# Group 2's mixer projection in feature pairs with the block operands beside it, group 0's final norm inside one projection, and the mixer constants at another address

## The chip, the cores and the metric

The kernel runs on one core of a Trainium2 chip. The metric is device time in microseconds from the start of one launch to its end. The kernel before was timed in three runs; a further execution was recorded by the hardware profiler, and it is that execution whose rows are shown here. Engines carry the profile's names: PE is TensorE (matmuls) and PEld its weight loads, DVE is VectorE, ACT is ScalarE, POOL is GpSimd, SPq is the queue in which SyncE issues DMAs.

## What is computed

The reference is one inference step of a two-layer decoder on 1040 prompt positions (16 learned meta tokens and 1024 own ones) and 8 decode tokens, with 1024 features. Layer 0 mixes tokens by a causal convolution, layer 1 by an RWKV-7 recurrence; each is followed by a squared-ReLU MLP with 4096 hidden features. Cut to what matters:

```python
def _trunk(h, ...):
    for i in range(DEPTH):                       # DEPTH = 2
        hn = _rmsnorm(h, norm_mix[i])
        if i % N_MIXERS == 0:
            out, buf = _conformer_conv(hn, ...)
        else:
            out, sh, S = _rwkv7(hn, ...)         # ends with ((yn + bonus) * g) @ w_o
        h = h + out
        h = h + _sqrelu_mlp(_rmsnorm(h, norm_mlp[i]), w_mlp_in[i], w_mlp_out[i])
    return _rmsnorm(h, norm_final), ...

def _sqrelu_mlp(h, w_in, w_out):
    return jnp.square(jax.nn.relu(h @ w_in)) @ w_out
```

The change touches what stands behind the recurrence: the projection by `w_o` with its residual add, the preparation of layer 1's MLP, the final norm of the first third of the positions, and the place in memory of some constants of layer 1's mixer.

## The kernel before

**Layout.** Features lie on the 128 partitions, in `KT` = 8 blocks, and tokens along the free axis. A product in full precision is three matmuls (`mm3`, lines 209 to 213): every operand is split into a high part (a cast on ACT, lines 159 and 177) and a low part (a subtraction, line 160 on DVE for activations, line 182 on POOL for weights in four pieces of 256). A dense product of one 128-feature column is 8 blocks times three, 24 matmuls.

**Stages.** Layer 0's convolution and MLP come first, then layer 1's mixer in four groups with its inputs (`mixer_in`), beside which a serial recurrence over 17 chunks runs. The rest works on three groups of positions, `G2` = 328, 352 and 352 wide, called 0, 1 and 2:

- `mixer_out(g)` (lines 1614 to 1627) loads the residual `h1` and the mixer's output `z` (eight `zr` loads, each split), takes eight weight columns of `w_o` one after the other, multiplies each with `z` into a bank `ps_oo`, adds the bank to the residual (line 1625), squares the sum for the norm (line 276), and calls `fill` in the middle of each column and after it, so that other work is woven in.
- Group 0 goes through `mixer_out(0)` and its own MLP (`mlp`), with the end of the recurrence woven in.
- Groups 1 and 2 go through `mixer_out(1)` and `mixer_out(2)` and then share one MLP, `strassen_mlp`, which computes a block of two hidden columns for two groups with seven half products in place of eight. Their operands are `b11` and `b21` (group 1's own activations) and `b22`, `n1`, `t2`, `t3`, `m4`, which `strassen_acts` forms from both groups' residuals (lines 1695 to 1721). The order of the products on PE is `a11` by `b11`, `a12` by `b21`, `s2` by `t2`, `n1` by `n1`, `s3` by `t3`, `s4` by `b22`, `a22` by `m4`. Each half product is 12 matmuls. The weight operands of a block come from `strassen_weights`, four DVE operations (lines 1730 to 1733).
- `strassen_acts` runs in program order after all of `mixer_out(2)`. For each of the four feature pairs (i, i + 4) it forms the four differences on DVE (lines 1711 to 1714), `b22` (1715 and 1716), and splits the four.
- `final(g)` is the final norm of a group: squares, a scaling by the norm's weights, row sums, and for every 128 positions eight transposes into two banks `pf` (line 1662), two evictions into an output tile `ot` (DVE line 1667, ACT line 1665) and one DMA. `final(0)` is woven into `mixer_out(1)` and `mixer_out(2)` by `filler(4 * KT, ..., FB)`, 32 points for a weight of `FB` = 40 units of which the generator has 22; its rest is drained after `mixer_out(2)`.

**What sets the order.** The program is traced in the order of the text and then placed by a planner that simulates the engines: each instruction has a priority by its place in the text, and the planner gives an engine the first one in priority that is ready in its simulated time. On the chip every engine and every DMA queue then works strictly in the planned order. So an instruction can be planned ahead of others that stand before it in the text; the operands of `strassen_acts` and the loads for `mixer_out` are such cases.

**Buffers.** Weight tiles as they come from memory (`raw`) rotate through a `Ring` of `raw_a` (2 buffers) and `raw_f` (3), and `ot` takes its tile from the same ring. PSUM banks at that point are six `mm`, one `w` (`psw2`) and one `x`; `final` uses `w` for both halves of a tile if the group is 0 or 1. Temporaries `t1` and `t2` have three buffers each. `residp` holds group 0's residual and is reused by `t3`; `actp2` holds group 2's `z` and is reused by `m4` and `b22`; `actp3` holds `n1` and `t2`. A pool that reuses an address waits for the last reader of what lay there.

**The mixer's constants.** The pool `mixc` (from line 787) holds `hsum`, `hsel`, `hspread`, `half`, `negs` and `omka`, 5.3 KB for a partition. It is opened first in the stack `ld`, ahead of `hnp` (`hx`, `xx`), `lorap`, `pr` and `mixp` (lines 819 to 822). When the mixer ends, `ld` is closed and the pools of the last stage are laid over it from the same lowest address, `raw_f` first.

Of the kernel before, what the change touches and what calls it, by code (L numbers as in the profile page):

```python
# [48 lines left out]
def hybrid_step(tc, x_prompt, x_sample, state_conv, state_shift, state_wkv, meta_tokens,  # L49
# [10 lines left out]
    with ctx:  # L60
# [724 lines left out]
        ld = ctx.enter_context(ExitStack())  # L785
        mixc = pool(ld, "mixc", 1)
# [32 lines left out]
        hnp = pool(ld, "hnp", 1)  # L819
        lorap = pool(ld, "lorap", 1)  # L820
        pr = pool(ld, "pr", 1)
        mixp = pool(ld, "mixp", 1)
# [777 lines left out]
        with ExitStack() as l1:  # L1600
# [13 lines left out]
            def mixer_out(g, residp, actp, fill, add):  # L1614
                lo, n = G2[g]
                h1 = hl[g] = residp.tile([P, KT, cur["wide"]], F32, name=f"h1_{g}", tag="h")
                nc.sync.dma_start(h1[:, :, :n], d_h[:, :, lo:lo + n])
                z = new_act(actp, f"z{g}", cur["wide"])
# [4 lines left out]
                for m in range(KT):  # L1623
                    ps = dense(load_col(rwkv_w_o[0], m, f"wo{g}_{m}", nc.gpsimd), z, n, f"oo{g}_{m}", fill)
                    nc.vector.tensor_add(h1[:, m, :n], h1[:, m, :n], ps[:, :n])
                    add(m, h1[:, m, :n])
                    fill()

            def final(g):
# [24 lines left out]
                for j, i in enumerate(starts):  # L1654
# [3 lines left out]
                    ot = cur["raw"].tile([P, D], F32, name=f"ot{g}_{i}", tag="raw")  # L1658
                    for hf in range(2):
                        pt = bank(f"pf{g}{i}{hf}", "w" if g < 2 or hf else "mm")  # L1660
# [34 lines left out]
            def strassen_acts(first, h2, n, own, shared, last):  # L1695

                ah, al, h1 = first[3], first[4], first[1]
                parts = {}
                for q, (pl, tag) in enumerate(((own, "t1"), (own, "t2"), (shared, "h"))):
                    t = pl.tile([P, KT, cur["wide"]], F32R, name=f"sa{q}", tag=tag)  # L1700
                    parts[q] = t[:, :HT, :n], t[:, HT:, :n]
                zh, zl = new_act(last, "sa3", cur["wide"])
                parts[3] = zh[:, :HT, :n], zl[:, :HT, :n]
                b22 = zh[:, HT:, :n], zl[:, HT:, :n]
                for i in range(HT):
                    lo, hi = h2[:, i, :], h2[:, HT + i, :]
                    x = tt(f"sx{i}", "t2")[:, :n]
                    nc.scalar.activation(x, lo, AF.Copy, scale=gam(i))
                    t = [tt(f"st{q}{i}", "t1")[:, :n] for q in range(3)] + [tt(f"st3{i}", "t2")[:, :n]]
                    stt = nc.vector.scalar_tensor_tensor  # L1710
                    stt(t[0], h1[:, i, :], gam(i), x, op0=ALU.mult, op1=ALU.subtract)
                    stt(t[2], hi, gam(HT + i), x, op0=ALU.mult, op1=ALU.subtract)
                    stt(t[1], hi, gam(HT + i), t[0], op0=ALU.mult, op1=ALU.add)
                    stt(t[3], h1[:, HT + i, :], gam(HT + i), t[1], op0=ALU.mult, op1=ALU.subtract)
                    nc.scalar.activation(b22[0][:, i], hi, AF.Copy, scale=gam(HT + i))
                    stt(b22[1][:, i], hi, gam(HT + i), b22[0][:, i].bitcast(F32), op0=ALU.mult, op1=ALU.subtract)
                    for q in range(4):
                        split(parts[q][0][:, i], parts[q][1][:, i], t[q], nc.vector)
                low = lambda k: [t[:, k:k + HT, :n] for t in (ah, al)]
                return dict(b11=low(0), b21=low(HT), b22=b22, n1=parts[0], t2=parts[1], t3=parts[2], m4=parts[3])  # L1720
# [112 lines left out]
            cur.update(rings((raw_a, raw_f), (wsp_a, wsp_f)))  # L1833
            cur["mm"] = Ring((cur["mm"], 4), (pool(lp, "psum2", 2, space=PSUM), 2))
# [6 lines left out]
            fill, rest = filler(4 * KT, ([ranked(FN, final(0))], FB))  # L1841
# [54 lines left out]
```

## Time and profile before

| what | value |
|---|---|
| three runs, median (lowest to highest) | 2796.94 us (2789.36 to 2797.69) |
| the profiled execution's own time | 2799.78 us |
| its span, on which all rows are placed | 2797.9 us |
| mean granted TensorE clock | 0.966 |
| busy POOL, share of the span | 1731.6 us, 62% |
| busy ACT, share of the span | 1405.6 us, 50% |
| DMA moved | 428.31 MB, mean 153 GB/s |

The times of rows are microseconds from the start of the span. A timeline row reads: start, length, engine, line, operation, output from inputs, shapes, count, and in brackets how long the engine had been idle and what released it. A row of consecutive instructions is merged, so a DMA issue of 24 us in the queue SPq is the time in which a run of issues held the queue, with their waits. A row of the groups reads: line, engine, operation, names, shapes, count, busy us, mean ns, and idle time before. Lines are those of helpers where a helper records the operation: 159 and 160 are `split`, 165 `load_raw`, 177 and 182 `load_w`, 211 to 213 `mm3`, 266 the sums of `mean_bcast`, 288 the accumulation of squares, 295 the reciprocal of `rstd_of`.

### The profile page before, as it was taken

Reading aid. Unit: us, or ns where it says so; the run is one execution under the profiler, and the core shown is the slowest. Engines: PE = TensorE matmul, PEld = TensorE weight load, DVE = VectorE, ACT = ScalarE, POOL = GpSimd, SP = SyncE. Lnnn points to the kernel's source line nnn. Section 1 sums busy time; section 2 is a strip of 40 time slices with the busy share of each in tenths; the row PEclk is TensorE's granted clock in tenths of the full one; section 3 lists DMA queues with packets and bytes.
Section 4 is the critical chain, followed back from the end, with each engine's and each line's share of the span. In section 5 each row is a group of like instructions: output and inputs, shape, how many; then the busy total and the mean of one; then the engine's idle time right before and its main releaser. Section 6 shows DMA issues by size and latency. Waiting matters only on the chain.

```text
span 2797.9 us, 54227 instructions
## 1 busy us (share of the span) xinstructions
PE 2603.5 (93%) x20362; PEld 2508.0 (90%) x20362; DVE 2050.5 (73%) x3860; ACT 1405.6 (50%) x2616; POOL 1731.6 (62%) x2287
## 2 busy tenths in 40 slices
PE   8998999999998999988898899878899989999998
PEld 7998999999998999978787788768889989999998
DVE  5999999996457464786888786777797667555565
ACT  5545444544355444565657666754444544333333
POOL 6686877887786354645434344647558775666563
PEclk9999999999999999999999899989999999999999
DMA  6573544454444556678878787796557452222221
GB/s 186 160 194 91 160 136 136 131 181 136 138 132 143 154 155 177 191 199 197 225 201 203 201 215 183 190 234 179 142 136 230 139 153 68 76 68 79 73 69 64
DMA packets 659284, 428.31 MB, mean 153 GB/s; under 512 B 126840, under 2 KB 609208, under 8 KB 659022
## 3 DMA queue, kind: packets, MB, share of 16 engines
q1 hardware_dynamic: 652780, 421.93, 54.2%
q10 hardware_dynamic: 6018, 2.89, 0.4%
q8 instruction: 160, 2.62, 0.4%
q14 instruction: 102, 0.84, 0.1%
q0 software_dynamic: 224, 0.03, 0.0%
HBM read 353.03 MB, written 72.66 MB: 152 GB/s over the span
## 4 chain that ended last, share of the span: by engine, by line
PE 61%; DVE 16%; DMA 8%; POOL 6%; ACT 5%; issue 4%; SPq 1%; ACTq 0%; POOLq 0%; DVEq 0%
PE out L212 4%; PE out L213 4%; PE out L211 4%; PE ps_in L212 4%; PE ps_in L213 4%; PE ps_in L211 4%; PE os L212 3%; PE os L213 3%; PE os L211 3%; POOL wo_lo L182 2%; POOL wi_lo L182 2%; PE su L211 1%; PE su L213 1%; PE su L212 1%; DVE cv L552 1%
## 5 line engine op out<-in xcount | busy, mean ns | idle before, releaser
L182 POOL TENSOR_TENSOR wo_lo<-wo_raw,wo_hi 128x256 fp32r<-128x256 f32 x544 | 427.9, 820 | 190.0 <-ACT wo_hi L177 176.9
L182 POOL TENSOR_TENSOR wi_lo<-wi_raw,wi_hi 128x256 fp32r<-128x256 f32 x472 | 366.1, 809 | 163.0 <-ACT wi_hi L177 160.5
L552 DVE SCALAR_TENSOR_TENSOR cv<-u,wdw,cv 128x352 f32<-128x352 f32 (+2 forms) x720 | 376.6, 572 | 0.7
L211 PE MATMUL out<-hh,wo_hi 128*128 128x348 f32 (+2 forms) x1024 | 335.1, 331 | 21.7 <-DVE h L382 9.1
L211 PE MATMUL ps_in<-m_h,wi_hi 128*128 128x348 f32 (+2 forms) x1024 | 330.4, 323 | 5.2 <-DVE h L382 3.1
L212 PE MATMUL out<-hh,wo_lo 128*128 128x348 f32 (+2 forms) x1024 | 332.5, 325 | 2.2 <-DVE wo_lo L182 2.2
L213 PE MATMUL out<-hl,wo_hi 128*128 128x348 f32 (+2 forms) x1024 | 328.7, 324 | 2.0 <-DVE hl L160 2.0
L212 PE MATMUL ps_in<-m_h,wi_lo 128*128 128x348 f32 (+2 forms) x1024 | 328.6, 322 | 0.9 <-POOL wi_lo L182 0.8
L213 PE MATMUL ps_in<-m_l,wi_hi 128*128 128x348 f32 (+2 forms) x1024 | 328.1, 321 | 0.2
L382 DVE TENSOR_TENSOR h<-h,out 128x348 f32<-128x348 f32 (+2 forms) x512 | 249.9, 503 | 66.5 <-PE out L213 66.4
L177 ACT CAST wo_hi<-wo_raw 128x1024 fp32r<-128x1024 f32 x152 | 159.2, 1049 | 207.3 <-PE ps_in L213 115.8
L177 ACT CAST wi_hi<-wi_raw 128x1024 fp32r<-128x1024 f32 x128 | 134.2, 1048 | 236.7 <-PE out L213 113.4
L211 PEld LDWEIGHTS out<-hh,wo_hi 128*128 128x128 f32 x1024 | 195.9, 192 | 30.1 <-DVE h L382 11.4
L211 PEld LDWEIGHTS ps_in<-m_h,wi_hi 128*128 128x128 f32 x1024 | 193.3, 189 | 8.4 <-issue 3.3
L212 PEld LDWEIGHTS out<-hh,wo_lo 128*128 128x128 f32 x1024 | 196.7, 192 | 4.2 <-DVE wo_lo L182 2.9
L213 PEld LDWEIGHTS out<-hl,wo_hi 128*128 128x128 f32 x1024 | 195.3, 192 | 3.2 <-DVE hl L160 2.7
L212 PEld LDWEIGHTS ps_in<-m_h,wi_lo 128*128 128x128 f32 x1024 | 193.0, 189 | 2.8 <-POOL wi_lo L182 1.7
L213 PEld LDWEIGHTS ps_in<-m_l,wi_hi 128*128 128x128 f32 x1024 | 192.3, 188 | 1.4 <-DVE m_l L305 0.7
L1803 DVE TENSOR_TENSOR h<-h,os 128x352 f32<-128x352 f32 x256 | 127.4, 515 | 57.9 <-PE os L213 57.2
L212 PE MATMUL os<-hhs,wos_lo 128*128 128x352 f32 x512 | 165.2, 323 | 0.0
L213 PE MATMUL os<-hls,wos_hi 128*128 128x352 f32 x512 | 164.2, 323 | 0.0
L211 PE MATMUL os<-hhs,wos_hi 128*128 128x352 f32 x512 | 156.1, 323 | 0.0
(498 smaller groups left out, 8036.1 us busy)
## 6 DMA issues: line engine op xcount, KB each, us to landing
wi_raw<-in_w_mlp_in_dram SPq DMA_DIRECT2D x128, 512.0 KB
wo_raw<-in_w_mlp_out_dram SPq DMA_DIRECT2D x128, 512.0 KB
wk_raw<-in_rwkv_w_k_dram SPq DMA_DIRECT2D x32, 512.0 KB
wr_raw<-in_rwkv_w_r_dram SPq DMA_DIRECT2D x32, 512.0 KB
wv_raw<-in_rwkv_w_v_dram SPq DMA_DIRECT2D x32, 512.0 KB
d_ab<-ab SPq DMA_DIRECT2D x32, 512.0 KB
ws_raw<-in_w_mlp_in_dram SPq DMA_DIRECT2D x32, 512.0 KB
wos_raw<-in_w_mlp_out_dram SPq DMA_DIRECT2D x32, 512.0 KB
```

The lines of the kernel that those rows point to most:

```text
L177: nc.scalar.copy(hi[:, :a * b], raw[:, :a * b])
L182: eng_lo.tensor_sub(lo[:, cs], raw[:, cs], hi[:, cs].bitcast(F32))
L211: nc.tensor.matmul(ps, w[0], act[0], start=first, stop=False, **kw)
L212: nc.tensor.matmul(ps, w[1], act[0], start=False, stop=False, **kw)
L213: nc.tensor.matmul(ps, w[0], act[1], start=False, stop=last, **kw)
L382: nc.vector.tensor_add(hv[:, 4 * i + m, :], hv[:, 4 * i + m, :], ps[:, :n])
L552: nc.vector.scalar_tensor_tensor(acc[m][:, :n], ug[:, m, j:j + n], wdw[:, m, j:j + 1], acc[m][:, :n], op0=ALU.mult, op1=ALU.add)
L1803: nc.vector.tensor_add(hv[:, 4 * i + m, :], hv[:, 4 * i + m, :], ps[:, :n])
```

## The change

It has three parts.

1. **Group 2's projection in pairs.** `mixer_out` takes an order of columns and a hook. For group 2 the order is 0, 4, 1, 5, 2, 6, 3, 7, nothing is woven in, and after the second column of each pair the hook forms `n1`, `t2`, `t3` for that pair. `strassen_acts` becomes two functions: `early`, the hook, and `late`, which after the norm's statistics forms `b22` and then `m4`. As the difference behind `t2` is no longer kept, `m4` starts from its two split parts, added on POOL.
2. **Group 0's final norm within `mixer_out(1)`.** The weaving has 16 points and a weight of 25, and the rest is drained right behind `mixer_out(1)`. Its output tiles come from a new pool `outp` with one buffer, and the first half of each tile's transposes uses the `mm` banks.
3. **Constants.** `hnp`, `lorap`, `pr` and `mixp` are opened ahead of `mixc`.

```diff
@@ the pools of the mixer
         ld = ctx.enter_context(ExitStack())
+        hnp = pool(ld, "hnp", 1)
+        lorap = pool(ld, "lorap", 1)
+        pr = pool(ld, "pr", 1)
+        mixp = pool(ld, "mixp", 1)
         mixc = pool(ld, "mixc", 1)
...
-        hnp = pool(ld, "hnp", 1)
-        lorap = pool(ld, "lorap", 1)
-        pr = pool(ld, "pr", 1)
-        mixp = pool(ld, "mixp", 1)
@@ mixer_out
-            def mixer_out(g, residp, actp, fill, add):
+            def mixer_out(g, residp, actp, fill, add, order=range(KT), early=None):
+                ready = None
...
+                if early:
+                    ready = early(h1)
...
-                for m in range(KT):
+                for i, m in enumerate(order):
                     ps = dense(load_col(rwkv_w_o[0], m, f"wo{g}_{m}", nc.gpsimd), z, n, f"oo{g}_{m}", fill)
                     nc.vector.tensor_add(h1[:, m, :n], h1[:, m, :n], ps[:, :n])
-                    add(m, h1[:, m, :n])
+                    add(i, h1[:, m, :n])
+                    if ready:
+                        ready(m)
                     fill()
@@ final
-                    ot = cur["raw"].tile([P, D], F32, name=f"ot{g}_{i}", tag="raw")
+                    ot = (cur["raw"] if g else outp).tile([P, D], F32, name=f"ot{g}_{i}", tag="raw")
                     for hf in range(2):
-                        pt = bank(f"pf{g}{i}{hf}", "w" if g < 2 or hf else "mm")
+                        pt = bank(f"pf{g}{i}{hf}", "w" if hf or g == 1 else "mm")
@@ strassen_acts, new
+                def early(h2):
+                    for q, pl, tag in (("n1", own, "t1"), ("t2", own, "t2"), ("t3", shared, "h")):
+                        room(q, pl, tag)
+
+                    def ready(m):
+                        if m < HT:
+                            return
+                        i = m - HT
+                        lo, hi = h2[:, i, :n], h2[:, m, :n]
+                        x = tt(f"sx{i}", "t2")[:, :n]
+                        nc.scalar.activation(x, lo, AF.Copy, scale=gam(i))
+                        t = {q: tt(f"st{q}{i}", "t1")[:, :n] for q in ("n1", "t2", "t3")}
+                        stt(t["n1"], h1[:, i, :], gam(i), x, op0=ALU.mult, op1=ALU.subtract)
+                        stt(t["t2"], hi, gam(m), t["n1"], op0=ALU.mult, op1=ALU.add)
+                        stt(t["t3"], hi, gam(m), x, op0=ALU.mult, op1=ALU.subtract)
+                        for q in t:
+                            split(ops[q][0][:, i], ops[q][1][:, i], t[q], nc.vector)
+                    return ready
+
+                def late(h2, pl):
+                    zh, zl = new_act(pl, "sa3", cur["wide"])
+                    ops["m4"] = zh[:, :HT, :n], zl[:, :HT, :n]
+                    b22 = ops["b22"] = zh[:, HT:, :n], zl[:, HT:, :n]
+                    for i in range(HT):
+                        hi = h2[:, HT + i, :n]
+                        nc.scalar.activation(b22[0][:, i], hi, AF.Copy, scale=gam(HT + i))
+                        stt(b22[1][:, i], hi, gam(HT + i), b22[0][:, i].bitcast(F32), op0=ALU.mult, op1=ALU.subtract)
+                    for i in range(HT):
+                        t4 = tt(f"st4{i}", "t2")[:, :n]
+                        nc.gpsimd.tensor_add(t4, ops["t2"][0][:, i].bitcast(F32), ops["t2"][1][:, i].bitcast(F32))
+                        stt(t4, h1[:, HT + i, :], gam(HT + i), t4, op0=ALU.mult, op1=ALU.subtract)
+                        split(ops["m4"][0][:, i], ops["m4"][1][:, i], t4, nc.vector)
+                return ops, early, late
@@ the last stage
+            outp = pool(l1, "outp", 1)
...
-            fill, rest = filler(4 * KT, ([ranked(FN, final(0))], FB))
+            fill, rest = filler(2 * KT, ([ranked(FN, final(0))], 25))
             add, sums = sums_of(1)
             mixer_out(1, residp2, actp, fill, add)
-            g1 = group(1, actp, hidp, sums)
-            add, sums = sums_of(2)
-            mixer_out(2, residp2, actp2, fill, add)
             for _ in rest:
                 pass
+            g1 = group(1, actp, hidp, sums)
             n = G2[2][1]
+            ops, early, late = strassen_acts(g1, n, actp3, residp)
+            add, sums = sums_of(2)
+            mixer_out(2, residp2, actp2, lambda: None, add, [m for i in range(HT) for m in (i, i + HT)], early)
             rs = rstd_of(mean_bcast(sums, n, "m12"), n, 0, "m12", "rsm", 2)
-            ops = strassen_acts(g1, hl[2][:, :, :n], n, actp3, residp, actp2)
+            late(hl[2], actp2)
```

More of the change, by code (lines that the diff above doesn't have):

```diff
@@ L1693, in hybrid_step, with strassen_acts, room @@
             gam = lambda k: vec("norm_mlp", KT + k)
-            def strassen_acts(first, h2, n, own, shared, last):
+            def strassen_acts(first, n, own, shared):
                 ah, al, h1 = first[3], first[4], first[1]
-                parts = {}
-                for q, (pl, tag) in enumerate(((own, "t1"), (own, "t2"), (shared, "h"))):
+                low = lambda k: [t[:, k:k + HT, :n] for t in (ah, al)]
+                ops = dict(b11=low(0), b21=low(HT))
+                stt = nc.vector.scalar_tensor_tensor
+                def room(q, pl, tag):
@@ L1700, in strassen_acts @@
                     t = pl.tile([P, KT, cur["wide"]], F32R, name=f"sa{q}", tag=tag)
[L1701 to L1718, printed above, removed]
@@ L1719, in strassen_acts @@
-                low = lambda k: [t[:, k:k + HT, :n] for t in (ah, al)]
-                return dict(b11=low(0), b21=low(HT), b22=b22, n1=parts[0], t2=parts[1], t3=parts[2], m4=parts[3])
+                    ops[q] = t[:, :HT, :n], t[:, HT:, :n]
+                def early(h2):
[15 more added lines that the diff above has]
+                    return ready
```

## The prediction

> **What bounds the kernel now.** The first view is the page: the head, the busy shares, the slices.
>
> ```profile
> span 2797.9 us, 54227 instructions
> ...
> PE 2603.5 (93%) x20362; PEld 2508.0 (90%) x20362; DVE 2050.5 (73%) x3860; ACT 1405.6 (50%) x2616; POOL 1731.6 (62%) x2287
> ...
> PE   8998999999998999988898899878899989999998
> ```
>
> TensorE is busy 93% of the span, and the change removes no matmul. So only the holes of TensorE beside the touched code can give time. A busy share hides part of a hole, because ends of matmuls are modelled and a matmul at half clock counts as busy; I therefore count matmuls per stretch. The second view is the table of windows, over the two places that the tail edits touch (columns: length, then busy us and count of PE, PEld, DVE, ACT, POOL, then the granted clock, DMA share, GB/s).
>
> ```profile
> 2244.00:2256.00 12.00, 9.10 (x41) 8.43 (x40) 4.06 (x6) 4.37 (x6) 6.21 (x9) 0.72 0.76 222
> ...
> 2300.00:2336.00 36.00, 27.58 (x129) 24.06 (x128) 30.70 (x44) 18.66 (x36) 20.23 (x23) 0.86 0.19 57
> 2336.00:2372.00 36.00, 36.00 (x227) 36.00 (x227) 25.08 (x42) 15.64 (x27) 24.97 (x31) 1.00 0.25 74
> ```
>
> The last row is full speed: 227 matmuls in 36 us, 0.159 us each. In 2300 to 2336 there are 129, 98 fewer: 98 x 0.159 = 15.6 us lost. Eight of the 129 are the slower sums of squares (rows under hole B: a pair takes 0.75 to 0.86 us with its end, two others 0.159 + 0.32), four pairs that take about 1 off: **15 us** in round. In 2244 to 2256 there are 41, eight of them transposes (row under hole A: 1.05 us for four): 33 x 0.159 + 2.1 = 7.3 us of work in 12, so **4.7 us** lost. The rest of the span after 2336 is full and is not touched.
>
> **Hole A, 2244 to 2256, and the first group's final norm.** The timelines of SyncE's queue and of TensorE name the cause.
>
> ```profile
> 2207.91 8.73 SPq L165 DMA_DIRECT2D wo_raw<-in_rwkv_w_o_dram  x3
> 2216.74 24.25 SPq L1621 DMA_DIRECT2D zr<-d_z  x14
> 2241.04 1.05 SPq L165 DMA_DIRECT2D wo_raw<-in_rwkv_w_o_dram  x2
> ...
> 2247.53 0.34 SPq L1669 DMA_DIRECT2D out_dram<-ot  x1
> ```
>
> ```profile
> 2246.97 0.66 PE L211 MATMUL ps_oo<-z_h,wo_hi 128*128 128x352 f32 x1 [2.76 <-ACT wo_hi L177]
> 2249.70 1.05 PE L1662 MATMUL pf<-ident,h 128*128 128x128 f32 x4
> ```
>
> The fifth weight column of group 1's projection is issued at 2241.04, behind fourteen `zr` loads that hold the in-order queue for 24.25 us, six of them group 2's. Its buffer comes from a ring of five, which in program order reads column 0, 1, 2, `ot`, 3, 4, `ot`, 5: the output tile `ot` takes a slot, so column 4 must wait until column 0's is free. The change gives the first group's `ot` a pool of its own (`outp`, one buffer). Column 4 then takes the fifth slot, and one reuse less stands before it; it ranks before group 2's `zr`, so the planner can issue it ahead of them. Moving the final norm's instructions removes and adds none: 24 transposes, six evictions and three output transfers stay; they are spread over 16 fill points at 25/16 instead of 32 at 40/32, so the first `ot` comes at fill point 5 instead of 6. Half of the transposes go to the `mm` banks instead of the single `w` bank.
>
> `outp` adds a wait: the second `ot` can be written only when the first transfer has landed. Behind that waiting eviction on VectorE and ScalarE stand the residual adds and weight casts. Tiles lie 5 units apart, at 25/16 per fill point 3.2 points, and a point is 12 matmuls, 1.9 us: 6.1 us apart. The nearest landings of 512 KB are these two in the chain.
>
> ```profile
> 2241.04 4.80 DMA wo_raw<-in_rwkv_w_o_dram
> ```
>
> ```profile
> 1838.15 7.33 DMA wo_raw<-in_rwkv_w_o_dram
> ```
>
> At 4.80 us the wait is nothing, at 7.33 it is 1.2 us twice, covered by free `mm` banks. So hole A is worth 0 (the order stays) to 4.7; I take **-4.5**, since the slot that blocked is the edit's own.
>
> **Hole B, 2300 to 2336, and the feature pairs.** The projection of group 2 ends at T = 2300.7, where the sums start.
>
> ```profile
> 2300.70 0.75 PE L266 MATMUL st_m<-acc_m,ones_d 128*128 128x352 f32 x2
> 2302.78 0.86 PE L266 MATMUL st_m<-acc_m,ones_d 128*128 128x352 f32 x2 [1.33 <-DVE acc_m L288]
> ...
> 2324.90 0.55 PE L211 MATMUL su<-sa,ws_hi 128*128 128x352 f32 x1
> ...
> 2334.91 0.43 PE L211 MATMUL su<-sa_h,wb_hi 128*128 128x352 f32 x1 [0.62 <-DVE u L1779]
> ```
>
> The third product of the block (`s2` by `t2`) starts at T + 24.2. By TensorE alone it could start after eight sums (about 2 us) and 24 matmuls (3.8): T + 5.8. VectorE, which forms the operands, has two holes before T and after them none that counts until 2327:
>
> ```profile
> 2278.26 0.65 DVE L1711 SCALAR_TENSOR_TENSOR st<-h,pvec,sx 128x352 f32<-128x352 f32 x1 [3.52 <-ACT sx L1708]
> ...
> 2286.96 1.08 DVE L1730 SCALAR_TENSOR_TENSOR wsa<-ws_raw 128x512 f32<-128x512 f32 x1 [4.54 <-POOL wo_lo L182]
> ...
> 2327.78 0.58 DVE L160 TENSOR_TENSOR hls<-p,hhs 128x352 fp32r<-128x352 f32 x1 [1.08 <-ACT hhs L159]
> ```
>
> That is 8.06 us free, because with columns in order 0 to 7 the first pair (0, 4) is complete only after five columns of 24 matmuls (3.8 us each). In order 0, 4, 1, 5, ... pairs are complete after 2, 4, 6, 8, so the first three are 11.4, 7.6 and 3.8 us earlier and fall into these gaps. What still ran on VectorE after 2300, from the groups by shape:
>
> ```profile
> L160 DVE TENSOR_TENSOR sa<-st,sa 128x352 fp32r<-128x352 f32 x9 | 6.0, 684 | 0.0
> L1716 DVE SCALAR_TENSOR_TENSOR sa_l<-h,pvec,sa_h 128x352 fp32r<-128x352 f32 x4 | 3.3, 815 | 0.0
> L160 DVE TENSOR_TENSOR sa_l<-st,sa_h 128x352 fp32r<-128x352 f32 x4 | 3.1, 784 | 0.0
> L295 DVE RECIPROCAL rs_m<-sd_m 128x352 f32<-128x352 f32 x1 | 2.3, 2339 | 0.0
> L1713 DVE SCALAR_TENSOR_TENSOR st<-h,pvec,st 128x352 f32<-128x352 f32 x3 | 2.2, 733 | 0.0
> L1714 DVE SCALAR_TENSOR_TENSOR st<-h,pvec,st 128x352 f32<-128x352 f32 x3 | 2.2, 726 | 0.0
> L1711 DVE SCALAR_TENSOR_TENSOR st<-h,pvec,sx 128x352 f32<-128x352 f32 x2 | 1.6, 806 | 0.0
> ...
> L1712 DVE SCALAR_TENSOR_TENSOR st<-h,pvec,sx 128x352 f32<-128x352 f32 x2 | 1.1, 571 | 0.0
> ```
>
> The first, fifth, seventh and eighth rows are `n1`, `t2`, `t3`: 16 instructions, 10.9 us. After the change the last pair alone is left, five instructions (its `n1` needs only column 3): 5 x 0.72 = 3.6 us, so `t2` is ready near T + 5 and the third product loses almost nothing. The late part then holds the end: 3.6, the reciprocal 2.3, `b22` 3.3, `m4` 3.1 + 4 x 0.73 = 6.0, and the first hidden tile's add, scale and split, about 2.2: 17.4 us, so `m4` near T + 18. Its product is due at T + 2 + 72 x 0.159 = T + 13.5. The gap of some 4.5 us can take 24 matmuls of the next block (3.8 us), as the trace does before. I leave 5 us of the 15: **-10**.
>
> ScalarE's count is unchanged. Four additions on GpSimd that rebuild `t2` are new, 1.2 us each by this row:
>
> ```profile
> L288 POOL TENSOR_TENSOR acc_m<-acc_m,sq 128x352 f32<-128x352 f32 x1 | 1.2, 1225 | 0.0
> ```
>
> They stand among the weight splits: 4.9 us, and behind them `wb_lo` and the next block's `wa_lo`. GpSimd's own timeline has a hole there:
>
> ```profile
> 2303.28 3.92 POOL L182 TENSOR_TENSOR wt_lo<-wsb,wt_hi 128x256 fp32r<-128x256 f32 x4
> 2312.06 2.02 POOL L182 TENSOR_TENSOR wb_lo<-ws_raw,wb_hi 128x256 fp32r<-128x256 f32 x2 [4.87 <-ACT wb_hi L177]
> ```
>
> Its 4.87 us are the cover; without it the last product waits up to 4.9 us.
>
> **The price of sharing.** The same operation costs twice as much while GpSimd works:
>
> ```profile
> 2293.64 1.06 DVE L1713 SCALAR_TENSOR_TENSOR st<-h,pvec,st 128x352 f32<-128x352 f32 x1
> ...
> 2308.16 0.57 DVE L1713 SCALAR_TENSOR_TENSOR st<-h,pvec,st 128x352 f32<-128x352 f32 x1
> ```
>
> GpSimd was splitting at 2293 and idle at 2308. Moved before T, all 24 operations can cost about 1 us. Eleven early ones more, at 1.0, are 11 us against 8.06 free; 3 us overflow past T, and up to 5 more where the late ones lose their quiet stretch. So B lies between -3 and -14.
> The Trainium skill says in "SBUF — State Buffer", section "Who interferes with whom", that a VectorE instruction with two SBUF inputs contends with a GpSimd instruction that reads SBUF, and that whichever starts first has the pair until it ends. The two rows above agree (1.06 against 0.57 us); by that rule every moved operation pays the long price, which is the second rival.
>
> **Part C, the mixer's constants.** Only addresses change: `mixc` (5.3 KB by its shapes) goes from below `hnp` to above `mixp`. The tail's first raw weight buffers reuse the lowest addresses. Before, they wait for the constants' last reader, after it for `hx`:
>
> ```profile
> L1135 PEld LDWEIGHTS pk<-rk,hsum x64: 186/189/394, 1162.0 to 1829.1; 128*128 128x128 f32 x64
> ```
>
> ```profile
> L890 DVE SCALAR_TENSOR_TENSOR mx<-xx,pvec,hx x96: 382/484/1282, 886.1 to 1750.4; 128x256 f32<-128x256 f32 x48, 128x272 f32<-128x272 f32 x24, 128x264 f32<-128x264 f32 x24
> ```
>
> So three loads can leave up to 79 us earlier. They now hold SyncE here:
>
> ```profile
> 1837.67 4.21 SPq L165 DMA_DIRECT2D wo_raw<-in_rwkv_w_o_dram  x3
> ```
>
> ```profile
> 1837.55 3.39 PE L1286 MATMUL A<-xa,bk 128*128 128x256 f32 x8 [7.84 <-DMA bk<-d_ab]
> ```
>
> TensorE's 7.84 us wait ends before these loads are issued, so it stays; behind them only SyncE's 4.21 us goes, from the gate operands' loads. I take **-2**, with -8 (wait and queue shortened) and +6 (one load in front of the chain, near the 7.33) as ends.
>
> **The sum.** The profiled execution takes 2799.78 us, its span of 2797.9 and 1.9 around it. 2799.8 - 4.5 - 10 - 2 = 2783.3. Its 2799.78 lies 2.84 above the median of the three runs, 2796.94 (2789.36 to 2797.69), so the median forecast is **2780**.
>
> **Rivals.** (1) *The queue order stays*: fourteen `zr` still hold SyncE, the same wait takes A's place. For it: the planner chose that order once; against: the freed slot. A = 0: 2785. (2) *VectorE remains the bound* through sharing: B = -3, A = -4.5, C = 0: 2789. For it: the doubled durations; against: the quiet 4.87 us. (3) *Both holes close and the mixer's end loosens*: -4.7 - 14 - 6 = -25: 2772. (4) *The change does not do what it says*: the planner had already drawn eleven operand operations before T, and gains nothing more: 2796. (5) *Slower*: the three early `wo_raw` loads are put ahead of the recurrence's loads in 1750 to 1830, in a serial chain. 3 x 7.33 = 22 us, and after each hole a lower clock as in hole A (0.72 over 12 us, at most 3.4 us, 2 taken) makes 28; with A and B, +13: 2810. It decides once more than 14.5 us of that delay reach the chain. For it: the DMA share of 1.00 in 1820 to 1860; against: the low rank of these loads.
>
> ```profile
> 1820.00:1860.00 40.00, 24.69 (x371) 20.09 (x370) 25.66 (x54) 23.05 (x53) 22.48 (x28) 0.83 1.00 273
> ```
>
> **How the numbers follow.** Forecast 0.42, rivals (1) 0.18, (2) 0.20, (3) 0.08, (4) 0.05, (5) 0.07. The bound of 0.3%, about what a measurement can tell from no change, is 8.4 us: faster means below 2788.5. The forecast but 0.02, rival (1) but 0.01, (3) and 0.08 of (2) are faster: 0.73; (5) is slower: 0.07; the rest 0.20. The range 2768 to 2793 leaves out half of (3), (4), (5) and a little of (2): under 0.2.
>
> **What would show it.** A: `wo_raw` for column 4 issued before group 2's `zr`, and some 75 matmuls in the 12 us where there were 41. B: `s2` by `t2` within 8 us of the last projection matmul instead of 24.2, and VectorE's two holes gone. C: `wo_raw` issued between 1750 and 1835. Wrong would be: VectorE without a gap yet ending as late after T; or a new wait of `ot` on its transfer; or group 0's projection starting later than before.

## The result and the profile after

| kernel | median (lowest to highest), runs | profiled execution, span |
|---|---|---|
| before | 2793.81 us (2789.36 to 2797.69), 4 | 2799.78 us, 2797.9 us |
| changed | 2773.59 us (2773.24 to 2776.21), 4 | 2773.24 us, 2771.5 us |

The ratio is 0.993, with a 95% interval of 0.9911 to 0.995: faster, by some 20 us. The execution of before whose rows were shown lies 6 us over its median, so the two traces are 26.5 us apart. The page of the changed kernel, its head, busy shares and TensorE's slices:

```profile
span 2771.5 us, 54241 instructions
...
PE 2596.3 (94%) x20362; PEld 2500.8 (90%) x20362; DVE 2064.6 (74%) x3860; ACT 1405.7 (51%) x2616; POOL 1738.0 (63%) x2291
...
PE   8998999999998999997898889979989999999998
```

TensorE has the same 20362 matmuls. VectorE has the same count too, yet 14.1 us more of busy time: its mean instruction became dearer. Most of that comes with part C: VectorE is busy 2060.9 to 2065.4 us in the traces with C and 2049.9 to 2054.7 in those without. The windows of the changed kernel over the two places (columns as before: length, busy us and count of PE, PEld, DVE, ACT, POOL, clock, DMA share, GB/s):

```profile
2212.00:2224.00 12.00, 12.00 (x84) 11.96 (x83) 8.73 (x14) 9.14 (x20) 9.72 (x12) 1.00 0.56 160
2224.00:2236.00 12.00, 12.00 (x82) 11.72 (x81) 8.51 (x14) 7.74 (x13) 10.73 (x13) 1.00 0.88 270
...
2276.00:2312.00 36.00, 27.27 (x147) 25.02 (x146) 32.18 (x42) 18.80 (x37) 26.78 (x29) 0.95 0.15 44
2312.00:2348.00 36.00, 34.49 (x216) 34.20 (x215) 21.61 (x40) 13.32 (x23) 23.04 (x28) 1.00 0.25 74
```

The first two rows are group 1's projection: where before had 41 matmuls at a clock of 0.72 there are now 84 and 82 at 1.00. Hole A is gone. The last two rows begin with the end of group 2's projection: 147 matmuls where before had 129, then 216 where before had 227. Hole B became shallower and longer. The cause of the first is in SyncE's queue:

```profile
2201.90 8.60 SPq L1624 DMA_DIRECT2D zr<-d_z  x6
2210.55 3.59 SPq L165 DMA_DIRECT2D wo_raw<-in_rwkv_w_o_dram  x2
2216.83 2.36 SPq L1624 DMA_DIRECT2D zr<-d_z  x3
```

The run of fourteen `zr` that held the queue for 24.25 us is broken up; six of group 1's `zr` are followed by two `wo_raw`, and only then come the next `zr`.

**Where the time went.** All fourteen traces of this study were cut at three points that every kernel has: the first matmul of group 0's projection (`ps_oo`), the last output matmul of group 0's MLP, and T, the last matmul of group 2's projection (2300.5 in before). Microseconds, worked out from the first and last starts of these tiles, good to 0.1:

| kernel | parts in it | first `ps_oo` at | to end of group 0's MLP | to T | T to end | `s2` by `t2`, after T |
|---|---|---|---|---|---|---|
| before | none | 1856.4 | 370.0 | 74.1 | 497.4 | 24.4 |
| changed | A B C | 1845.3 | 363.5 | 66.8 | 495.9 | 12.6 |
| `only_a` | A | 1844.7 | 365.0 | 66.8 | 492.8 | 20.6 |
| `only_b` | B | 1852.8 | 367.7 | 73.3 | 495.7 | 15.2 |
| `only_c` | C | 1844.8 | 361.6 | 72.9 | 498.5 | 25.1 |
| `a_and_b` | A B | 1853.0 | 367.5 | 66.8 | 494.7 | 13.5 |
| `a_and_c` | A C | 1849.0 | 364.9 | 66.8 | 492.9 | 20.6 |
| `b_and_c` | B C | 1840.6 | 360.4 | 73.6 | 496.0 | 15.6 |

The 26.4 us are 11.1 ahead of group 0's projection, 6.5 in its MLP, 7.3 on the way to T, and 1.5 behind T. So part C, which was priced at 2 us, and part A carry the result; part B, priced at 10, nearly nothing.

How far one trace can be trusted shows in the last stretch: `before` and `only_c`, the changed kernel and `a_and_b`, `only_b` and `b_and_c`, `only_a` and `a_and_c` each share TensorE's planned order behind T, and the two of a pair lie 1.1, 1.2, 0.3 and 0.1 us apart there. The 1.5 us behind T are hardly more than that.

### The profile page after: what moved, and what is told of

It is laid out like the page before. It is cut to its first block, busy times and chain, and to the rows that moved or that the text cites. A ratio compares the mean times of both kernels' runs of the same rounds, so it can differ in the third digit from the quotient of the medians.

```text
span 2771.5 us, 54241 instructions
## 1 busy us (share of the span) xinstructions
PE 2596.3 (94%) x20362; PEld 2500.8 (90%) x20362; DVE 2064.6 (74%) x3860; ACT 1405.7 (51%) x2616; POOL 1738.0 (63%) x2291
## 4 chain that ended last, share of the span: by engine, by line
PE 62%; DVE 17%; DMA 9%; issue 4%; ACT 4%; POOL 3%; SPq 1%; POOLq 0%; ACTq 0%; DVEq 0%
PE ps_in L212 5%; PE ps_in L213 4%; PE out L212 4%; PE ps_in L211 4%; PE out L213 4%; PE out L211 4%; PE os L211 3%; PE os L213 3%; PE os L212 3%; DVE cv L552 2%; PE su L213 1%; PE su L212 1%; PE su L211 1%; PE A L1286 1%; DMA wr_raw<-in_rwkv_w_r_dram 1%
## 5 line engine op out<-in xcount | busy, mean ns | idle before, releaser
L211 PE MATMUL out<-hh,wo_hi 128*128 128x348 f32 (+2 forms) x1024 | 332.8, 328 | 18.7 <-DVE h L382 7.7
```

The source lines that it names most:

```text
L211: nc.tensor.matmul(ps, w[0], act[0], start=first, stop=False, **kw)
```

## The experiments

### Each part alone, and each left out

`only_c` moves the four pools ahead of `mixc`. All kernels made for this study drain the rest of group 0's final norm right behind `mixer_out(1)`, as the changed kernel does and before doesn't, also those called without A. That alone is small: to T the kernels without a piece of A take 72.9 to 73.6 us, before 74.1. `only_a` is before with the new pool, the banks and the weaving:

```diff
-                    ot = cur["raw"].tile([P, D], F32, name=f"ot{g}_{i}", tag="raw")
+                    ot = (cur["raw"] if g else outp).tile([P, D], F32, name=f"ot{g}_{i}", tag="raw")
...
-                        pt = bank(f"pf{g}{i}{hf}", "w" if g < 2 or hf else "mm")
+                        pt = bank(f"pf{g}{i}{hf}", "w" if hf or g == 1 else "mm")
...
+            outp = pool(l1, "outp", 1)
...
-            fill, rest = filler(4 * KT, ([ranked(FN, final(0))], FB))
+            fill, rest = filler(2 * KT, ([ranked(FN, final(0))], 25))
```

`only_b` has the pair order with `early` and `late` and nothing else. `a_and_b` is the changed kernel with the pools in their old order, `a_and_c` the changed kernel with the old `strassen_acts` and its call, `b_and_c` the changed kernel with `ot` in the ring, the old banks and the old weaving.

> The kernel before with part C alone, the constants above mixp. Theory of the two traces: the address change brings most of the gain, because group 0's projection started 11.1 us earlier and its sums 14.5 us earlier: 2793.8 - 14 = 2780 us, with the first ps_oo near 1845. Rival, the sizes of the prediction: C brings 2 us, 2792, and the early stages owe their shift to chance in one profiled execution. Second rival, the parts do not add: anything between, with holes A and B unlike both kernels.

> The kernel before with part A alone: group 0's final norm with its own output pool, mm banks and 16 weaving points. Theory of the two traces: between the end of group 0's MLP and the end of group 2's projection 7.4 us went, so 2793.8 - 6 = 2788 us, with the load of column 4 ahead of group 2's zr and no wait of PE on a weight cast there. Rival, the queue order stays: 2793 us and the wait of 2.8 us is still there.

> The kernel before with part B alone: feature pairs, early and late operands. Theory of the two traces: from the end of the projection to the first product of s2 by t2 it is still 19 us, VectorE is the bound, and B brings 1 to 2 us: 2792 us. Rival, the size of the prediction: B brings 10 us, 2784 us, and its loss in the changed kernel comes from meeting A or C.

> The changed kernel with the pools of the mixer in the old order, so A and B without C. Theory of the two traces, with parts that add: 2793.8 - 6 - 1.5 = 2786 us. If C brings only 2 us, as the prediction has it: 2776 us. If the parts do not add, it lies apart from the sum of only_a and only_b by more than 4 us.

> The changed kernel with the projection of group 2 and the operands as before, so A and C without B. Theory: only_a and a_and_b say that the feature pairs cost some 3 us once the final norm is out of the way (492.8 us from the last projection matmul to the end without them, 494.7 with them), because VectorE is bound before and after T; then this beats the changed kernel by 2 to 5 us, 2770 us. Rival, B is worth its 1 to 2 us here as well: 2775 us.

> The changed kernel with group 0's final norm as before, so B and C without A. Theory of parts that add: the stretch from the end of group 0's MLP to the last projection matmul is 73 us in the kernels without A and 66.8 in those with it, so this loses 6 to 7 us against the changed kernel: 2780 us. Rival, A owes its gain to chance in the early stages: 2774 us, and the stretch is 67 us here.

Measured, each against runs of before taken beside it:

| kernel | median us, runs | before us | ratio, 95% |
|---|---|---|---|
| `only_c` | 2781.11, 6 | 2791.64 | 0.9955, 0.9937 to 0.9972 |
| `only_a` | 2778.33, 6 | 2791.64 | 0.9948, 0.9933 to 0.9963 |
| `only_b` | 2790.25, 12 | 2791.64 | 0.9993, 0.9982 to 1.0004 |
| `a_and_b` | 2784.59, 12 | 2791.64 | 0.9975, 0.9966 to 0.9984 |
| `a_and_c` | 2771.96, 6 | 2793.29 | 0.9924, 0.9908 to 0.9939 |
| `b_and_c` | 2777.34, 6 | 2793.29 | 0.9948, 0.9928 to 0.9969 |

A alone and C alone are each faster, B alone can't be told from before. `only_c`, `only_b` and `b_and_c` came within 3 us of their first theory; `only_a` came 10 us below its 2788, in part for a reason behind T that is told below. The saving of `a_and_b` is 7.7 us less than the sum of those of `only_a` and `only_b` (7.05 against 13.31 and 1.39), so A and B don't add. The intervals of `a_and_b` and `only_a` don't meet: B put on top of A alone made the kernel slower. Behind T the traces give it 1.9 us there (494.7 against 492.8), and 3.0 with C present (495.9 against 492.9); the rest of the 6.3 us between the two medians I can't place. `a_and_c`, without B, can't be told from the changed kernel.

**What A does** is the same in every trace that has it: 66.8 us to T where the others have 72.9 to 74.1. The timeline of TensorE in `only_a` at this place holds no wait, and SyncE's queue there is that of the changed kernel.

**What C does** shows as one wait. In each of the six traces without C (before, `only_a`, `only_b`, `a_and_b` and two kernels below) TensorE waits 7.2 to 8.0 us for `bk`, a load of the recurrence. Before's row is in the prediction; the one of `only_a`:

```profile
1824.97 3.75 PE L1286 MATMUL A<-xa,bk 128*128 128x256 f32 x8 [7.47 <-DMA bk<-d_ab]
```

In none of the eight traces with C is this wait there. The timelines of SyncE, before first, then the changed kernel:

```profile
1830.73 0.52 SPq L1271 DMA_DIRECT2D bk<-d_ab  x1
```

```profile
1799.90 0.52 SPq L1271 DMA_DIRECT2D bk<-d_ab  x1
...
1813.35 5.04 SPq L165 DMA_DIRECT2D wo_raw<-in_rwkv_w_o_dram  x4
...
1834.22 0.63 SPq L1271 DMA_DIRECT2D bk<-d_ab  x1
```

and TensorE of the changed kernel:

```profile
1818.14 1.97 PE L1286 MATMUL A<-xa,bk 128*128 128x256 f32 x8 [1.16 <-DVE nr L1294]
...
1845.31 0.64 PE L211 MATMUL ps_oo<-z_h,wo_hi 128*128 128x328 f32 x1 [11.33 <-ACT z_h L159]
...
1853.48 1.89 PE L1286 MATMUL A<-xa,bk 128*128 128x256 f32 x8
```

The planner put the recurrence's steps in another order. TensorE's order is one and the same in all eight traces with C up to group 1's projection, and it parts from before's as early as 549 us, in layer 0. The `bk` loads issued from 1834.22 feed an `A` at 1853.48, which stands behind the first matmuls of group 0's projection; in before the `A` that waits for the loads of 1830.73 stands ahead of them. Ahead of the first `ps_oo` there are 208 matmuls into `A` without C and 192 with it, and 13974 against 13786 matmuls in all. What is late next is the projection's own operand: 11.33 us for `z`.

So an earlier first `ps_oo` is in part only work that now stands behind it, and the fairer cut runs from the mixer's start (the first `mx`, its token shift) to the end of group 0's MLP, which holds the same work in both orders (11756 matmuls, 11762 with all of A): 1310 to 1325 us in the eight traces with C, 1328 to 1340 in the six without. The start of the mixer is 2 to 5 us later with C than in before. Group 0's MLP stage, though 188 matmuls longer with C, takes 363.5 us in the mean (360.4 to 366.8) against 367.3 without (365.0 to 370.0). TensorE waits for `bk` at other places too, in every trace. Its waits for it in all (total us, times, longest), before and then the changed kernel:

```profile
PE A L1286 <- DMA bk<-d_ab: 18.2, 5, 7.8
```

```profile
PE A L1286 <- DMA bk<-d_ab: 8.4, 5, 3.7
```

They are 17.1 to 24.7 us in the six traces without C and 7.4 to 12.7 in the eight with it. That these waits are what pays is read from the traces; no run changes them alone, and the order differs in much else.

### The two halves of A

`outp_only` has the pool without the rest of A, but for the drain; `pace_bank` the weaving and the banks, with `ot` still in the ring.

```diff
@@ outp_only
-                    ot = cur["raw"].tile([P, D], F32, name=f"ot{g}_{i}", tag="raw")
+                    ot = (cur["raw"] if g else outp).tile([P, D], F32, name=f"ot{g}_{i}", tag="raw")
+            outp = pool(l1, "outp", 1)
@@ pace_bank
-                        pt = bank(f"pf{g}{i}{hf}", "w" if g < 2 or hf else "mm")
+                        pt = bank(f"pf{g}{i}{hf}", "w" if hf or g == 1 else "mm")
-            fill, rest = filler(4 * KT, ([ranked(FN, final(0))], FB))
+            fill, rest = filler(2 * KT, ([ranked(FN, final(0))], 25))
```

> The kernel before with one piece of part A: group 0's output tiles from their own pool, banks and weaving points as before. Theory of the prediction: the slot in the ring of raw weights is what blocked, so the stretch from the end of group 0's MLP to the last projection matmul falls from 73 to 67 or 68 us, 2786 us. Rival, the single w bank or the slower weaving was the cause: the stretch stays at 72 us or more, 2791 us.

> The kernel before with the other pieces of part A: 16 weaving points at 25 and the mm banks, output tiles in the ring of raw weights as before. From the end of group 0's MLP to the last projection matmul it was 74.1 us before, 70.0 with the own pool alone, 66.8 with all of A. Theory, two causes that add: 70 to 71 us here. Rival, the ring slot is the only one that counts and 66.8 owes its rest to the order: 73 to 74 us, and the wait for the weight cast is still there.

`outp_only`: 2786.2 us (11 runs) against 2793.29, ratio 0.9972 (0.9963 to 0.9981). `pace_bank`: 2795.12 us (12 runs) against 2792.79, ratio 1.0001 (0.9989 to 1.0014). From the end of group 0's MLP to T the first takes 70.0 us, the second 83.9, more than before. SyncE's queue in `pace_bank`, then in `outp_only`:

```profile
2190.14 14.43 SPq L165 DMA_DIRECT2D wo_raw<-in_rwkv_w_o_dram  x3
2204.66 27.12 SPq L1624 DMA_DIRECT2D zr<-d_z  x14
2231.83 1.05 SPq L165 DMA_DIRECT2D wo_raw<-in_rwkv_w_o_dram  x2
```

```profile
2197.78 15.69 SPq L165 DMA_DIRECT2D wo_raw<-in_rwkv_w_o_dram  x5
2213.52 1.05 SPq L1624 DMA_DIRECT2D zr<-d_z  x2
2215.89 0.38 SPq L165 DMA_DIRECT2D wo_raw<-in_rwkv_w_o_dram  x1
2216.32 8.01 SPq L1624 DMA_DIRECT2D zr<-d_z  x5
2224.39 0.42 SPq L165 DMA_DIRECT2D wo_raw<-in_rwkv_w_o_dram  x1
```

With `ot` in the ring three weight columns go out and then all fourteen `zr`, now for 27.12 us; with the pool five columns go out first and the `zr` stand between single columns. So the freed slot is what mends the queue. The weaving and the banks alone bring the `ot` tiles earlier into the ring and make the hole deeper; on top of the pool they are worth the other 3.2 us (70.0 to 66.8). Both results lie outside what was expected, the 70.0 between 67 or 68 and 72, the 83.9 far above 74.

What the pool lacks alone shows in `outp_only`, on VectorE and then on TensorE:

```profile
2251.34 0.75 DVE L1672 TENSOR_SCALAR ot<-pf,os 128x512 f32<-128x512 f32 x1 [1.58 <-DMA out_dram<-ot]
```

```profile
2252.15 0.66 PE L1667 MATMUL pf<-ident,h 128*128 128x128 f32 x4 [1.23 <-DVE ot L1672]
```

The second output tile waits for the transfer of the first, and TensorE's next transposes wait for its eviction, since the one `w` bank is still full. In all of A the same wait stands on VectorE and ScalarE, and TensorE, which has the `mm` banks besides, has none.

### What holds the end after T

Three kernels change only where B's work stands. In `held` the planner may not issue `late`, nor the second block's weight operands (`strassen_weights`, block 1, with its four sums), before the last `early` split. `held_pool` adds a move of five instructions from VectorE to GpSimd: the low parts of `m4` and one weight sum. `hold_late` holds `late` only.

```diff
@@ held
+            with tc.issue_after(tail["early"].ins):
-            late(hl[2], actp2)
+                late(hl[2], actp2)
...
+                    with ExitStack() as held:
+                        if b == 1:
+                            held.enter_context(tc.issue_after(tail["early"].ins))
+                        w = strassen_weights(2 * b)
@@ held_pool, besides
-                        split(ops["m4"][0][:, i], ops["m4"][1][:, i], t4, nc.vector)
+                        split(ops["m4"][0][:, i], ops["m4"][1][:, i], t4, nc.gpsimd)
-                v.tensor_sub(s3, a11, a21)
+                (nc.gpsimd if j == 2 else v).tensor_sub(s3, a11, a21)
```

> The changed kernel, with the late operands and the second block's weight sums tied behind the last early operand on VectorE; nothing else. Theory: hole B stays because the planner puts that later work ahead of the last pair, since it reckons without the doubled durations beside GpSimd; then t2 is ready some 9 us after T instead of 19, and 3 to 6 us go: 2769 us. Rival, VectorE is bound by the amount of its work and not by its order: the wait moves to b22, m4 or the next block, 2773 to 2776 us.

> The kernel held, with five operations taken from VectorE to GpSimd: the four low parts of m4 and one weight difference (s3) of the second block. Theory: after T VectorE is bound by the amount of its work; held only moved the wait from t2 to the next operands. Then some 3 us less on VectorE shorten the time from the last projection matmul to the end from 493.8 to 491 us or less. Rival, GpSimd's own weight splits are the bound there and it has no room: 494 us or more.

> The kernel held without its second tie: the late operands stay behind the last early operand, the second block's weight sums are free. In held PE waited 2.5 us on the second block's ws_lo, whose sums had been tied. Theory: that wait goes, t2 is some 3 us later, and the sum from T to the end falls below 493.8. Rival, every VectorE operation moved ahead delays another by as much: 493.8 within 0.5.

| kernel | median us, runs | before us | ratio, 95% | T to end | `s2` by `t2`, after T |
|---|---|---|---|---|---|
| `held` | 2767.5, 6 | 2793.29 | 0.991, 0.9891 to 0.9929 | 493.9 | 9.6 |
| `held_pool` | 2770.12, 6 | 2792.79 | 0.9916, 0.9901 to 0.9932 | 496.1 | 10.5 |
| `hold_late` | 2772.25, 6 | 2792.79 | 0.992, 0.9901 to 0.994 | 495.8 | 12.1 |

`held` brings `t2` forward: the last early split starts at T + 8.7 instead of T + 19.1. Behind T it gains 2.0 us on the changed kernel and 0.8 on `a_and_b`, which has the changed kernel's order there; neither the 3 to 6 us of its theory nor the nothing of its rival. `hold_late`, without the tie of the weight sums, gains nothing there, and missed both of its expectations. The median of `held` is the lowest of the kernels that compute the whole, but its interval overlaps that of the changed kernel (0.9911 to 0.995), so it isn't shown to be the better one. TensorE's waits in `held`:

```profile
2296.54 0.43 PE L211 MATMUL sv<-sa_h,wt_hi 128*128 128x352 f32 x1 [0.84 <-ACT p L1799]
2300.86 0.43 PE L211 MATMUL su<-sat,wt_hi 128*128 128x352 f32 x1 [1.96 <-ACT u L1794]
...
2306.20 0.42 PE L212 MATMUL sv<-san,ws_lo 128*128 128x352 f32 x1 [2.49 <-POOL ws_lo L182]
```

The wait for `t2` is gone, and 5.29 us of waits stand at the evictions and the second block's weights instead: the held instructions are late now. `held_pool` shows that GpSimd can't take them. Its window of 36 us from T, and its wait for the same weights:

```profile
2272.40:2308.40 36.00, 28.46 (x143) 25.25 (x142) 29.64 (x36) 18.04 (x36) 33.31 (x35) 0.91 0.14 45
```

```profile
2299.82 0.66 PE L212 MATMUL sv<-san,ws_lo 128*128 128x352 f32 x1 [2.32 <-POOL ws_lo L182]
```

VectorE falls to 29.64 of 36 us, GpSimd rises to 33.31, and TensorE has 143 matmuls, fewer than the changed kernel's 148 in its 36 us from T.

The last kernel takes work away instead of moving it. `no_low` is the changed kernel in which the low parts of `b22` and `m4` aren't formed.

```diff
-                    ops["m4"] = zh[:, :HT, :n], zl[:, :HT, :n]
-                    b22 = ops["b22"] = zh[:, HT:, :n], zl[:, HT:, :n]
+                    ops["m4"] = zh[:, :HT, :n], zh[:, :HT, :n]
+                    b22 = ops["b22"] = zh[:, HT:, :n], zh[:, HT:, :n]
...
-                        stt(b22[1][:, i], hi, gam(HT + i), b22[0][:, i].bitcast(F32), op0=ALU.mult, op1=ALU.subtract)
...
-                        split(ops["m4"][0][:, i], ops["m4"][1][:, i], t4, nc.vector)
+                        nc.scalar.copy(ops["m4"][0][:, i], t4)
```

> The changed kernel, but in the late part the low parts of b22 and m4 are not formed on VectorE: the products read the high part in their place. This leaves out eight VectorE instructions behind T (the last matmul group of the projection), 3.4 + 3.4 = 6.8 us by their two groups in the changed kernel; the matmuls stay as many. Theory: VectorE's sum of work behind T sets how long TensorE is held up there, so most of the 6.8 us come back: from T to the end 490 to 492.5 us where the changed kernel has 495.9, over 165 matmuls in the 36 us behind T where it has 148, median 2766 to 2770. Rival: TensorE waits for the order in which single operands come (t2's last pair, the next block's weights), not for VectorE's sum: from T to the end 495 to 496, the count within 145 to 152, median 2771 to 2775.

2763.06 us (4 runs) against 2793.49, ratio 0.9889 (0.9872 to 0.9907). From T to the end it takes 490.5 us: 5.4 of the 6.8 us came back. Its two windows from T (2270.1):

```profile
2270.10:2306.10 36.00, 30.92 (x172) 28.82 (x171) 29.90 (x36) 20.81 (x40) 29.87 (x35) 0.95 0.17 51
2306.10:2342.10 36.00, 36.00 (x226) 36.00 (x226) 24.38 (x46) 14.48 (x24) 23.35 (x28) 1.00 0.28 82
```

172 matmuls instead of 148, and the second window full, as that theory expected; the rival's 495 to 496 fell. So work taken off VectorE there comes back as time. It doesn't show that the sum of that work, and not its order, is what counts. The first product with `t2` starts no earlier (T + 14.0 against T + 12.6), but the last splits do:

```profile
2284.89 0.95 DVE L160 TENSOR_TENSOR sat<-stt,sat 128x352 fp32r<-128x352 f32 x2
```

They stand at T + 14.8, where the changed kernel has them at T + 18.7, and TensorE's wait for them is gone. And `only_a` speaks against the sum. In the 36 us behind T it starts 24 of VectorE's operand instructions (differences and low parts) and the changed kernel 20, and yet its time behind T is 3.1 us shorter. Its 36 us from T:

```profile
2276.50:2312.50 36.00, 28.91 (x155) 25.89 (x154) 31.93 (x47) 19.98 (x40) 22.26 (x25) 0.95 0.17 50
```

VectorE gets 47 instructions done in 31.93 us busy, 0.68 us each; the changed kernel's 42 take 32.18, 0.77 each. GpSimd is busy 22.26 us here and 26.78 there, about the four additions that part B puts on it (1.2 us each). So with B fewer of VectorE's instructions stand behind T and each is dearer: the 24 take 18.0 us, the 20 take 17.5. Which share of the 3.1 us this has, and which the order, no run tells apart.

## Why the prediction came out as it did

The total was right: 2773.59 us against 2780, within the range, and faster. None of the three sizes behind it was: A and C brought more than their terms, B nearly nothing, and the errors made up for each other. That the sum came out is luck.

**Hole A (-4.5): right in mechanism, too small.** `wo_raw` left ahead of group 2's `zr`, as stated, and the 12 us hold 82 to 84 matmuls (75 were expected). The stretch to T is 7.3 us shorter, since I counted only one 12 us window and the stretch lost time beside it too. Two things the term didn't have. The pool alone gives 4.1 of it, the pacing and banks the rest, which I had taken as free of effect. And in every kernel with a piece of A and without B the time from T to the end fell to 492.8 to 493.1, from 497.4 and 498.5, even in `pace_bank`. The planner's order behind T comes out another way there; which instruction in it is worth the 4.6 us isn't isolated. Part of it may be TensorE's clock: over the 36 us behind T the granted clock is 0.86 in before and `only_c`, 0.95 in `only_a` and `a_and_c`, 1.00 in `outp_only` and `pace_bank`. The feared wait of `ot` for its transfer is there, too. In the changed kernel VectorE waits 1.40 us for it and ScalarE 0.73 and 0.79, near the 1.2 that were reckoned; between 2200 and T TensorE waits for nothing. Rival (1), the same queue order, fell.

**Hole B (-10): the step "so `t2` is ready near T + 5" failed.** The pairs did bring the start of the product forward, from T + 24.4 to T + 12.6, but not to T + 5; and it starts on the pairs that are ready, the last piece of `t2` comes only at T + 19.2. VectorE's two holes ahead of T, 8.06 us, shrank to 1.42, 0.55 and 1.11 us. I had left five instructions of `n1`, `t2` and `t3` behind T. From the changed kernel's groups on VectorE in 2275 to 2312:

```profile
L1741 DVE SCALAR_TENSOR_TENSOR st<-h,pvec,st 128x352 f32<-128x352 f32 x4 | 4.2, 1054 | 0.0
...
L160 DVE TENSOR_TENSOR sat<-stt,sat 128x352 fp32r<-128x352 f32 x4 | 3.0, 780 | 0.0
```

Four splits of `t2` and `t3` still run behind T, not two; with them eight instructions of the three operands stand there, 6.4 us by their groups, where I had 3.6. And the sums for `m4` take 1054 ns each in the mean, where I had 0.73 us. Of all operand instructions 26 start in the 36 us behind T in before, 18.6 us of work, and in the changed kernel 20, still 17.5. The order of VectorE's timeline says why:

```profile
2277.92 0.51 DVE L1628 TENSOR_TENSOR h<-h,ps_oo 128x352 f32<-128x352 f32 x1
2278.35 0.98 DVE L1753 SCALAR_TENSOR_TENSOR wsa<-ws_raw 128x512 f32<-128x512 f32 x1
2279.36 1.31 DVE L1754 SCALAR_TENSOR_TENSOR wsa<-wsa,ws_raw 128x512 f32<-128x512 f32 x1
2280.60 1.06 DVE L1741 SCALAR_TENSOR_TENSOR st<-h,pvec,st 128x352 f32<-128x352 f32 x1
...
2284.53 0.51 DVE L1628 TENSOR_TENSOR h<-h,ps_oo 128x352 f32<-128x352 f32 x1
2284.96 0.57 DVE L1737 SCALAR_TENSOR_TENSOR sa_l<-h,pvec,sa_h 128x352 fp32r<-128x352 f32 x1
...
2293.32 1.04 DVE L1737 SCALAR_TENSOR_TENSOR sa_l<-h,pvec,sa_h 128x352 fp32r<-128x352 f32 x1
2294.28 0.95 DVE L160 TENSOR_TENSOR sat<-stt,sat 128x352 fp32r<-128x352 f32 x2
```

There is no gap in it, nor in the rows left out, and the last low part of `m4` ends at T + 25.9; in before it was T + 25.2, in the forecast T + 18. The planner drew the next block's weight sums (lines 1753 and 1754) and `m4` (1741) ahead of the residual add of the last feature: that add starts at 2284.53, 8.9 us after T (in before 10.1), and the sums of squares and the last pair wait behind it. TensorE's timeline:

```profile
2279.01 0.86 PE L266 MATMUL st_m<-sq,ones_d 128*128 128x352 f32 x2 [1.58 <-ACT sq L276]
...
2286.34 0.86 PE L266 MATMUL st_m<-sq,ones_d 128*128 128x352 f32 x2 [2.14 <-ACT sq L276]
...
2294.85 0.59 PE L213 MATMUL su<-sat,ws_hi 128*128 128x352 f32 x1 [4.43 <-DVE sat L160]
```

The wait for the operands hasn't gone; it moved to the last matmul of the third product. So the mark "VectorE without a gap yet ending as late after T", which I had named as the sign of being wrong, is what came, and rival (2), VectorE remains the bound through sharing, was nearest about this hole with -1.5 where it had -3 (its total of 2789 wasn't, because of A and C). What B is worth depends on A: behind T it takes off 1.4 to 2.8 us without A, and adds 1.8 to 3.1 with it. `held` tells that another order gives 0.8 to 2.0 us back, `no_low` that less work on VectorE gives 5.4 of 6.8 back.

The price of sharing that the rival named stands in the rows: the same operation, the low part of `b22` (line 1737), takes 0.57 us at 2284.96, in a gap of GpSimd, and 1.04 us at 2293.32, while GpSimd splits weights. GpSimd's timeline in the changed kernel:

```profile
2286.67 1.16 POOL L1740 TENSOR_TENSOR st<-sat 128x352 f32<-128x352 f32 x1 [2.44 <-DVE stt L1725]
...
2289.92 4.06 POOL L182 TENSOR_TENSOR wa_lo<-ws_raw,wa_hi 128x256 fp32r<-128x256 f32 x4
```

The Trainium skill says in "SBUF — State Buffer", section "Who interferes with whom", that VectorE and GpSimd share a port pair under an exclusive lock; the trace agrees in the longer time beside GpSimd, 1.04 against 0.57 us, and doesn't show the lock itself. The four additions on GpSimd that rebuild `t2` did find their cover: none of TensorE's three waits above is for GpSimd. But they fill part of the quiet stretch in which VectorE's work was cheap; that price stood in the range ("up to 5 more where the late ones lose their quiet stretch") and not in the -10. For more than them there is no room, as `held_pool` showed.

**Part C (-2): the step "TensorE's 7.84 us wait ends before these loads are issued, so it stays" failed.** I reasoned on a fixed order of instructions in which only the starts of three loads move. But the planner places all instructions anew, and in the order that all kernels with C share the step that waited for `bk` stands elsewhere. From the mixer's start to the end of group 0's MLP the mean falls from 1333.8 to 1318.4 us, 15 us, and nearly 4 of them are lost again by a later start of the mixer (889.8 against 886.0 in the mean). The runs give 10.5 us for C alone (2791.64 - 2781.11), outside my bounds of -8 to +6. The mark, `wo_raw` issued between 1750 and 1835, came true for all eight loads (the last at 1826.34, where before had three by 1820.87 and the other five from 1835.77 to 1848.91), and it wasn't the reason I had given. Rival (5), `wo_raw` ahead of the recurrence, fell: the projection started earlier in all eight traces with C than in before (1840.6 to 1849.0 against 1856.4), and C alone is faster.

**The sum.** Rival (3), at 2772, has the nearest number, but its mechanism isn't what happened: hole B didn't close.

## What to carry to other kernels

When an operand comes late because an in-order engine is full, forming it earlier may only reorder that engine's work: before counting the wait as gain, find out when its last piece will be ready in the planned order, and price the engine's work beside its neighbours, with what the edit itself adds to them. A run of loads that holds a queue is mended by the buffer that its victim waits for, and pacing without that buffer can make it worse. Where a planner places the program, an edit of addresses is an edit of the order; price it by the waits that stand near it, in both directions, and not as the move of single loads.

## What had not been expected of the hardware

Executions of one planned order differ by much in the recurrence. Before, `only_a`, `only_b`, `a_and_b`, `outp_only` and `pace_bank` share TensorE's planned order up to group 1's projection, and yet group 0's projection starts between 1844.7 and 1856.4 us in their traces, 11.7 us apart, while the stretch to T after an edit repeats to 0.1 us (66.8 in all kernels with the whole of part A) and the one behind T to 1.2. So a gain of a few microseconds was read from the stage it belongs to, and whole spans were not compared from one trace to another.
